# A pooling and SwiGLU layer on one core: all rows of x loaded first, still products on TensorE, low parts of the window means by TensorE and ScalarE

## The chip, the core and the metric

The kernel runs on one NeuronCore of a Trainium2 chip. The metric is the time of one execution on the device, in microseconds (us): the median of several executions. The engines are TensorE (PE; its weight loads are listed apart as PEld), VectorE (DVE), ScalarE (ACT), GpSimd (POOL) and SyncE (SP), which only issues transfers. A transfer (DMA) can be issued by SyncE or by GpSimd.

## The reference, cut to what matters

One layer is computed (DEPTH is 1, so the mixer is the pooling one, and the context tokens are never needed). x is 1024 x 1024, the hidden width F is 2816, everything is float32.

```
s_c = silu(c)
sh1, sc1, g1, sh2, sc2, g2 = split(s_c @ mod_w + mod_b, 6)
hx = x * (1 + sc1) + sh1
p_g = centred_window_mean(hx_g, w) - hx_g          # w = 2, 4, 8, 16; 256 columns each
ox = concat_g(p_g @ pool_w[g]) * pool_scale
x = layer_norm(ALPHA * x + g1 * ox, ln_g[0], ln_b[0])
h = x * (1 + sc2) + sh2
gt, up = split(h @ ffn_w_in, 2)
x = layer_norm(ALPHA * x + g2 * ((silu(gt) * up) @ ffn_w_out), ln_g[1], ln_b[1])
```

mod_w is 1024 x 6144, in six parts of 1024 columns (4 MB each) that the text calls by their names: sh1, sc1, g1, sh2, sc2, g2.

## The kernel before, in words

**Precision.** A product that has to keep float32 accuracy is made in one of two ways. A float32 product goes over TensorE in two passes (two matmul records for each). Or both operands are split into a high part, rounded to fp32r, and a low part, the rest; then three fp32r products of one pass each are summed (`mm3`, L260). `take_hi` (L265) makes a high part on ScalarE, `take_lo` (L268) the low part on VectorE by subtracting the high part.

**The front of the kernel** is everything ahead of the first product of the SwiGLU part (`gate_step`, L760). It goes as follows. The rows of x are in blocks of 128, `x0` to `x7`; `ORDER` puts blocks 1, 2, 3, 4 in half 0 and 5, 6, 7, 0 in half 1.

- *Window means.* For each half and each of 8 column blocks, `pool_inner` (L460) makes four float32 products of a block of x with a band matrix from the constants, and `pool_outer` (L465) one with the few halo rows, all into one PSUM bank (`ps_pt`). This gives mean minus row, transposed. `pool_hi` (L470, ScalarE) and `pool_lo` (L473, VectorE) then split the bank into `pt` high and low.
- *Row vectors of c.* A part of mod_w comes in eight slices of 128 x 1024 (`mod_load`, L294). VectorE adds slice times silu(c) into `acc` (`mod_add`, L490; the first of a part L488). Then eight narrow float32 products turn `acc` into a column (`mod_col`, L505), or two 512-wide ones spread it over all partitions (`g1_bank`, L547). Slices listed in `by_tensor` skip VectorE and go through TensorE as they are (`mod_whole`, L505).
- *Weights.* g1 times pool_scale, times 1 + sc1, is multiplied into pool_w on VectorE (`pool_w_weigh`, L569) and the result split (`wpsh`, `wpsl`).
- *Sums.* `pooled` (L261 to L263) makes for each block of rows and half of the columns 12 fp32r products of 256 columns: 16 such sums. `residual` (L607, VectorE) adds ALPHA x and frees the bank. Then per block: `mean`, `spread` (L628, ScalarE), `factor`, `norm` (L644, ScalarE), and `keep_row` stores the row.
- *Turning.* With all four blocks of half 0 normed, `turned` (L693) transposes them, `scaled_h` (L698, ScalarE) applies sc2 and sh2, `hidden_hi` and `hidden_lo` split. sc2 and sh2 are made as above (`finish_gain`, `finish_shift`, L675 to L680).
- *Gate.* `gate_load` brings slices of ffn_w_in, `gate_hi` (ScalarE) and `gate_lo` (VectorE) split them, and `gate_step` starts: 88 steps of six 512-wide fp32r products.

Behind the front come the rest of the SwiGLU part and the output products, by a long stream of 512-wide fp32r products that only TensorE bounds.

**What sets the order.** Each step is a job; `ORDER_OF_ISSUE` (L43) is a table that names the jobs in the order in which they are issued, and each engine runs its own instructions in that order. `PLACE_OF` (L111) says for each tile which buffer it takes, so which older tile must be done first. SyncE's queue runs in order as well: eight transfers are on their way at most, since each issue waits for the landing of the one eight places earlier. `warm_up` (L316) runs 12 float32 products of 128 columns on ones, ahead of everything.

Of the kernel before, what the change touches and what calls it, by code (L numbers as in the profile page):

```python
# [12 lines left out]
F32 = mybir.dt.float32  # L13
# [4 lines left out]
P = 128  # L18
# [14 lines left out]
WARM = 12  # L33
G2_AT = 5
BY_TENSOR = (0, 7)
# [28 lines left out]
gate_load.0 gate_load.1 gate_load.2 gate_load.3 gate_load.4 gate_load.5 pool_hi.10 pool_hi.8 mod_add.19 pool_inner.47
pool_outer.11 pool_inner.38 pool_hi.11 pool_inner.62 pool_inner.58 residual.1 pool_hi.9 mean.0 pooled.6 mod_add.20
pool_hi.14 spread.0 mod_add.21 residual.6 mod_add.22 pooled.4 pool_hi.15 factor.0 mod_col.1 mod_add.23 norm.0
residual.4 keep_row.0 mod_add.24 pooled.2 finish_gain.0 pooled.5 residual.2 mod_add.25 pooled.3 residual.5 residual.3
pooled.7 mean.2 mean.1 spread.2 mod_add.26 mod_whole.1 residual.7 spread.1 mean.3 factor.2 mod_whole.2 mod_add.27
norm.2 mod_add.28 pool_inner.48 spread.3 keep_row.2 pool_inner.49 pool_inner.51 pool_outer.12 pool_inner.50 factor.1
mod_col.2 pool_lo.10 norm.1 factor.3 pool_lo.11 norm.3 keep_row.1 pool_lo.14 pool_inner.52 pool_inner.53 turned.2  # L70
gate_hi.0 finish_shift.0 keep_row.3 turned.4 pool_lo.8 turned.3 scaled_h.2 pool_lo.9 turned.1 scaled_h.4 gate_lo.0
pool_inner.54 turned.0 turned.6 scaled_h.3 turned.7 scaled_h.0 pool_lo.15 turned.5 scaled_h.1 pooled.8 scaled_h.5
scaled_h.6 pooled.10 scaled_h.7 residual.8 hidden_hi.0 pooled.12 residual.10 gate_hi.2 hidden_lo.0 pooled.14
hidden_hi.1 residual.12 gate_hi.1 pool_inner.55 gate_lo.2 pool_outer.13 gate_step.0 gate_hi.4 residual.14 gate_step.1
# [1327 lines left out]
```

## Time and profile before

| | us |
|---|---|
| median of 3 runs | 742.33 (741.07 to 743.72) |
| profiled execution | 743.44 |
| its span, first to last instruction | 741.7 |
| TensorE busy in the span | 723.3 (98%) |
| VectorE, ScalarE, GpSimd busy | 556.9, 274.9, 171.9 |
| first gate product starts | 89.34 |
| last product of TensorE ends | 733.3 |
| mean granted TensorE clock | 0.971 |

How to read it: the page of the profile shows the span in 40 slices; TensorE is busy in nine tenths and more of all but the first slices. What matters for this change is the time before the first gate product, and there the stretches (busy time of an engine between two times, with the granted clock) and the timeline (instructions in order of time, merged where alike) are the views to use. The granted clock is 1.00 at 2.4 GHz and 0.50 at 1.2 GHz.

### The profile page before, as it was taken

To read this page: it belongs to the slowest core of one execution; us is meant where nothing else is said; L and a number is where in the kernel's file an instruction comes from. 1 tells how busy PE (TensorE), PEld (TensorE's weight loads), DVE (VectorE), ACT (ScalarE), POOL (GpSimd) and SP (SyncE) were. 2 spreads that over 40 slices of the span, in tenths; PEclk is the share of its full clock that TensorE was granted. 3 is DMA by queue.
4 is the path that set the end of the run, shared out by engine and by line. 5 is a ranking of instruction groups with operands and counts; after the bars stand their busy time and mean duration, and the time that the engine had idled before them with its cause. 6 is when DMAs were issued, how large, how long until landed. Compare 5 with 4: busy or idle time off the path is not lost.

```text
span 741.7 us, 9158 instructions
## 1 busy us (share of the span) xinstructions
PE 723.3 (98%) x3342; PEld 602.3 (81%) x3342; DVE 556.9 (75%) x677; ACT 274.9 (37%) x356; POOL 171.9 (23%) x131
## 2 busy tenths in 40 slices
PE   6999999999999999999999999999999999999995
PEld 5689988788888888888888888888888888888884
DVE  3788874749534788999999777975878679657896
ACT  0225954597441311311312212212557334335521
POOL 0000000005205835373733634600000000233100
PEclk7579999999999999999999999999999999999998
DMA  7999349566829589797987797456799856999612
GB/s 293 346 407 370 146 167 356 197 226 199 273 116 308 189 264 263 183 322 245 311 262 193 241 276 205 156 192 220 266 371 391 296 194 227 254 290 292 184 57 113
DMA packets 115202, 182.85 MB, mean 247 GB/s; under 512 B 7723, under 2 KB 66547, under 8 KB 114902
## 3 DMA queue, kind: packets, MB, share of 16 engines
q1 hardware_dynamic: 107894, 164.97, 64.4%
q0 software_dynamic: 7264, 17.30, 11.7%
q8 instruction: 26, 0.43, 0.2%
q14 instruction: 18, 0.15, 0.1%
HBM read 142.14 MB, written 51.64 MB: 261 GB/s over the span
## 4 chain that ended last, share of the span: by engine, by line
PE 92%; DMA 5%; DVE 2%; ACT 1%; issue 0%; SPq 0%; POOL 0%; POOLq 0%
PE ps_v L894 40%; PE ps_x L1105 16%; PE ps_gate L760 13%; PE ps_y L1105 12%; DMA wi<-in_ffn_w_in 2%; PE ps_pt L460 2%; PE ps_col L505 2%; PE ps_ox L261 1%; PE ps_ox L263 1%; PE ps_ox L262 1%; PE ps_h L693 1%; DMA x<-in_x 1%; DMA mw<-in_mod_w 1%; PE ps_pt L465 1%; DMA consts<-in_consts 1%; PE ps_psc L540 1%
## 5 line engine op out<-in xcount | busy, mean ns | idle before, releaser
L760 PE MATMUL ps_gate<-h,wih 128*128 128x512 f32 x352 | 109.3, 391 | 0.0
L894 PE MATMUL ps_v<-t,w0h 128*128 128x512 f32 x352 | 109.2, 391 | 0.0
L266 ACT CAST yhi<-yraw 128x1024 fp32r<-128x1024 f32 x77 | 78.7, 1051 | 79.6 <-DMA yraw<-in_ffn_w_out 17.0
L269 DVE TENSOR_TENSOR ylo<-yraw,yhi 128x1024 fp32r<-128x1024 f32 x77 | 91.6, 1219 | 18.2 <-ACT yhi L266 7.4
L961 POOL TENSOR_TENSOR s<-raw,raw 128x512 f32<-128x512 f32 x22 | 33.1, 1504 | 311.0 <-DMA raw<-in_ffn_w_in 301.9
L917 ACT ACTIVATE a<-a 128x512 f32<-128x512 f32 x22 | 13.9, 632 | 225.0 <-DVE a L916 225.0
L894 PEld LDWEIGHTS ps_v<-t,w0h 128*128 128x128 f32 x352 | 66.1, 188 | 14.5 <-issue 1.0
L760 PEld LDWEIGHTS ps_gate<-h,wih 128*128 128x128 f32 x352 | 65.7, 188 | 13.8 <-issue 0.5
L760 PE MATMUL ps_gate<-h,wil 128*128 128x512 f32 x176 | 68.5, 389 | 0.0
L894 PE MATMUL ps_v<-t,w0l 128*128 128x512 f32 x176 | 68.5, 389 | 0.0
L1105 PE MATMUL ps_x<-yhi 128*128 128x512 f32 x176 | 68.5, 389 | 0.0
L1105 PE MATMUL ps_x<-ylo,yhi 128*128 128x512 f32 x176 | 68.5, 389 | 0.0
L1105 PE MATMUL ps_x<-yhi,ylo 128*128 128x512 f32 x176 | 68.5, 389 | 0.0
L490 DVE SCALAR_TENSOR_TENSOR acc<-mw,s_col,acc 128x1024 f32<-128x1024 f32 x41 | 54.5, 1331 | 16.1 <-DMA mw<-in_mod_w 15.7
L1067 POOL DMA_DIRECT2D yraw<-in_ffn_w_out x22 | 18.7, 849 | 193.4 <-DMA yraw<-in_ffn_w_out 161.1
L894 PE MATMUL ps_v<-t,ws 128*128 128x512 f32 x264 | 63.4, 389 | 0.0
L894 PEld LDWEIGHTS ps_v<-t,ws 128*128 128x128 f32 x264 | 49.6, 188 | 10.3
L894 PE MATMUL ps_v<-h,w1h 128*128 128x512 f32 x176 | 54.2, 389 | 0.0
L894 PE MATMUL ps_v<-t,w1h 128*128 128x512 f32 x176 | 54.2, 389 | 0.0
L1105 PE MATMUL ps_y<-yhi 128*128 128x512 f32 x132 | 51.3, 389 | 0.0
L1105 PE MATMUL ps_y<-ylo,yhi 128*128 128x512 f32 x132 | 51.3, 389 | 0.0
L1105 PE MATMUL ps_y<-yhi,ylo 128*128 128x512 f32 x132 | 51.3, 389 | 0.0
(160 smaller groups left out, 1390.6 us busy)
## 6 DMA issues: line engine op xcount, KB each, us to landing
mw<-in_mod_w SPq DMA_DIRECT2D x48, 512.0 KB, 8.7
raw<-in_ffn_w_in SPq DMA_DIRECT2D x88, 256.0 KB, 5.6
wi<-in_ffn_w_in SPq DMA_DIRECT2D x22, 512.0 KB, 6.3
yraw<-in_ffn_w_out SPq DMA_DIRECT2D x44, 256.0 KB, 4.8
yraw<-ed SPq DMA_DIRECT2D x33, 256.0 KB, 6.0
ed<-in_ffn_w_out POOLq DMA_DIRECT2D x6, 1024.0 KB, 10.5
pd<-pk SPq DMA_DIRECT2D x11, 512.0 KB, 4.6
gd<-gk SPq DMA_DIRECT2D x11, 512.0 KB, 4.7
```

Of the source, the lines that this page charges most:

```text
L261: nc.tensor.matmul(ps, lh, rh, start=first, stop=False)
L266: nc.scalar.copy(hi, src)
L269: nc.vector.tensor_tensor(lo, src, hi.bitcast(F32), ALU.subtract)
L460: nc.tensor.matmul(pt_bank[half, ct][:, a:b], xr[ORDER[half][n]][:, ct * P : (ct + 1) * P], operand, start=n == 0, stop=False, skip_group_ ...
L490: nc.vector.scalar_tensor_tensor(acc, w, s_col[:, k : k + 1], acc, ALU.mult, ALU.add)
L505: nc.tensor.matmul(tiles["ps_col", j][:, n * WIDE : (n + 1) * WIDE], t[:, n * P : (n + 1) * P], by, start=first and n == 0, stop=last and ...
L760: nc.tensor.matmul(ps, x, y, start=k == n == 0, stop=k % 4 == 3 and n == 2, skip_group_check=k > 3)
L894: nc.tensor.matmul(ps, x, y, start=fresh and first, stop=last, skip_group_check=not fresh)
L917: nc.scalar.activation(a[:, 1], a[:, 1], ACT.Silu)
L961: nc.gpsimd.tensor_tensor(s, up1, up2, ALU.add)
L1067: nc.gpsimd.dma_start(raw[n][:, 1], ADDED[n // PAIRS](n % PAIRS), accum_op=ALU.add)
L1105: nc.tensor.matmul(ps, s[x][:, r * P : (r + 1) * P], t[y][:, d], start=fresh and j == m == 0, stop=j == PAIRS - 1 and m == 2, skip_group_c ...
```

## The change

All eight blocks of x are now loaded at the start, in turn with the slices of g1; then sc1, sc2 and sh2 follow. The small vectors, constants and halo rows move from SyncE's queue to GpSimd's. The warm-up becomes 64 fp32r products of 256 columns on a tile of ones (`still`), and 12 jobs `keep_warm` of four such products each stand among the first sums; their results are not used. The low part of all 16 window means is now made without VectorE: TensorE subtracts the high part in PSUM by a 512-wide fp32r product with a negated identity (`pool_less`), and ScalarE copies the rest out (`pool_rest`). pool_w is multiplied by g1 first (`pool_w_gain`, in two tiles of 128 x 256 for each job), and 1 + sc1 goes into the split (`pool_w_hi` on ScalarE, `pool_w_lo` on VectorE), 256 columns at a time. Slices 6 and 7 of sc1 now go through TensorE; slice 0 of sc2 and of sh2 no longer does. The table of the order and the table of buffers are new throughout, and all 16 `pooled` sums now stand ahead of the first `gate_step` (before: 12). The buffers that the later part takes in turn are sorted by when they were last used.

```diff
-WARM = 12
+WARM = 64
-BY_TENSOR = (0, 7)
+BY_TENSOR = (7,)
+LOW_BY_TENSOR = ((0, 1, 2, 3, 4, 5, 6, 7), (0, 1, 2, 3, 4, 5, 6, 7))
 ORDER_OF_ISSUE = """
-vector_rows.0 fill_constants.0 fill_ones.0 mod_start.0 warm_up.0 mod_load.0 load_consts.0 mod_load.1 load_x.0
...
+vector_rows.0 fill_constants.0 fill_ones.0 load_x.0 mod_start.0 negate.0 warm_up.0 load_consts.0 mod_load.0 load_x.1
...
+    minus = keep.tile([P, P], F32R, tag="minus", name="minus", bufs=1)
+    still = keep.tile([P, 256], F32R, tag="still", name="still", bufs=1)
...
         for _ in range(WARM):
-            nc.tensor.matmul(ps[:, :P], ones, ones, start=True, stop=True)
+            nc.tensor.matmul(ps[:, :256], still[:, :P], still, start=True, stop=True)
+    def keep_warm(n):
+        ps = bank(f"ps_still{n}")
+        for _ in range(4):
+            nc.tensor.matmul(ps[:, :256], still[:, :P], still, start=True, stop=True)
...
     def vector_rows(a, b, src):
-        nc.sync.dma_start(rows[a:b, :], src.rearrange("(j p) -> j p", p=P))
+        (nc.gpsimd if a else nc.sync).dma_start(rows[a:b, :], src.rearrange("(j p) -> j p", p=P))
...
+    def negate():
+        nc.scalar.activation(minus, ident, ACT.Copy, scale=-1.0)
+    def pool_less(half, ct):
+        nc.tensor.matmul(pt_bank[half, ct], minus, pt[half](0, ct), start=False, stop=True, skip_group_check=True)
+    def pool_rest(half, ct):
+        nc.scalar.copy(pt[half](1, ct), pt_bank.pop((half, ct)))
...
-    mod_columns(SC1, ())
+    mod_columns(SC1, (6, 7))
...
-    def pool_w_weigh(n):
+    def pool_w_gain(n):
+        w, g = tiles["wp", n // 2][:, n % 2 * 2 : n % 2 * 2 + 2, :], tiles["g1",][:, n * 256 : (n + 1) * 256]
+        for k in range(2):
+            nc.vector.tensor_tensor(w[:, k], w[:, k], g, ALU.mult)
+    def pool_w_hi(n):
+        nc.scalar.activation(wps[n // 4][0][:, n % 4], tiles["wp", n // 4][:, n % 4], ACT.Copy, scale=sc1[:, n : n + 1])
+    def pool_w_lo(n):
+        nc.vector.scalar_tensor_tensor(lo, tiles["wp", n // 4][:, n % 4], sc1[:, n : n + 1], hi.bitcast(F32), ALU.mult,
+                                       ALU.subtract)
...
-    mod_columns(SC2, (0,))
+    mod_columns(SC2, ())
```

What the tables do is seen in the rows of each engine. First SyncE's queue from its start, before (`mw_1_0` is slice 0 of sc1, `mw_2_0` slice 0 of g1, `x1` a block of x):

```order
L337 DMA rows_66<-in_c 8x128
L382 DMA acc2_156<-in_mod_b 1x1024
L294 DMA mw_1_0_172<-in_mod_w 128x1024
L356 DMA consts_72<-in_consts 128x288
L294 DMA mw_1_1_175<-in_mod_w 128x1024
L353 DMA x1_177<-in_x 128x1024
L294 DMA mw_1_2_179<-in_mod_w 128x1024
L337 DMA rows_66<-in_mod_b 48x128
L337 DMA rows_66<-in_ln_g 8x128
L337 DMA rows_66<-in_ln_b 8x128
L353 DMA x2_190<-in_x 128x1024
L294 DMA mw_1_3_192<-in_mod_w 128x1024
```

The same queue after the change:

```order
L353 DMA rows_66<-in_c 8x128
L369 DMA x1_159<-in_x 128x1024
L372 DMA consts_74<-in_consts 128x288
L301 DMA mw_2_0_231<-in_mod_w 128x1024
L369 DMA x2_233<-in_x 128x1024
L301 DMA mw_2_1_237<-in_mod_w 128x1024
L369 DMA x3_240<-in_x 128x1024
L301 DMA mw_2_2_243<-in_mod_w 128x1024
L369 DMA x4_246<-in_x 128x1024
L301 DMA mw_2_3_251<-in_mod_w 128x1024
L369 DMA x5_253<-in_x 128x1024
```

x and g1 alternate, sc1 has moved behind both, and the small rows are gone from this queue. Next TensorE near the end of the means of half 0, before (`ps_pt0_7` is the bank of half 0, column block 7; `x3`, `x4` are blocks of half 0, `x5` of half 1):

```order
L460 MATMUL ps_pt0_7_271<-consts_72,x3_194 128x143
L460 MATMUL ps_pt0_7_271<-consts_72,x4_199 128x135
L465 MATMUL ps_pt0_7_271<-consts_72,halo_207 128x2x8
L547 MATMUL ps_g1_0_375<-acc2_156,ones_69 128x512
L547 MATMUL ps_g1_1_381<-acc2_156,ones_69 128x512
L460 MATMUL ps_pt1_7_387<-consts_72,x5_263 128x136
L460 MATMUL ps_pt1_3_390<-consts_72,x5_263 128x130
```

The same place after it (L500 is `pool_inner`, L505 `pool_outer`, L517 `pool_less`, L336 `keep_warm`):

```order
L517 MATMUL ps_pt0_2_295<-pt0_01_328,minus_70 128x512
L517 MATMUL ps_pt0_1_274<-pt0_00_323,minus_70 128x512
L517 MATMUL ps_pt0_4_337<-pt0_02_361,minus_70 128x512
L500 MATMUL ps_pt0_5_353<-consts_74,x2_233 128x135
L500 MATMUL ps_pt0_5_353<-consts_74,x3_240 128x135
L500 MATMUL ps_pt0_5_353<-consts_74,x4_246 128x131
L505 MATMUL ps_pt0_5_353<-consts_74,halo_248 128x2x8
L336 MATMUL ps_still0_376<-still_71 128x256 x4
L336 MATMUL ps_still1_383<-still_71 128x256 x4
L500 MATMUL ps_pt1_7_390<-consts_74,x5_253 128x136
```

The 512-wide subtractions and the still products stand among the narrow window products, and the sums of g1 come later. Last ScalarE around its first weights of the gate (`wih0_0`), before:

```order
L628 ACTIVATE sq4_659,mv4_528<-x4_199,mv4_528 128x1024
L629 ACTIVATE mv4_528<-mv4_528,eps_70 128x1
L644 ACTIVATE x2_190<-x2_190,mv2_593 128x1024
L644 ACTIVATE x4_199<-x4_199,mv4_528 128x1024
L266 CAST wih0_0_697<-wi_0_0_482 128x1024
L698 ACTIVATE h32_0_1_715<-ps_h0_2_692,shift_75,gain_74 128x512
```

After it (L273 is `take_hi`, L690 the `spread`, L706 the `norm`):

```order
L520 CAST pt1_10_668<-ps_pt1_1_411 128x512
L273 CAST wih0_0_815<-wi_0_0_685 128x1024
L690 ACTIVATE sq4_834,mv4_739<-x4_246,mv4_739 128x1024
L691 ACT_TABLE_LOAD
L691 ACTIVATE mv4_739<-mv4_739,eps_72 128x1
L690 ACTIVATE sq1_866,mv1_688<-x1_159,mv1_688 128x1024
L691 ACTIVATE mv1_688<-mv1_688,eps_72 128x1
L690 ACTIVATE sq2_893,mv2_670<-x2_233,mv2_670 128x1024
```

The cast of the first gate weights now stands ahead of all four spreads of half 0, where it stood behind their norms.

## Rows read from the trace of the kernel before

**Rows 1.** Stretches of TensorE: from:to us, busy (instructions), granted clock, DMA share, GB/s

```profile
89.34:101.70 12.36, 12.36 (x55) 1.00 0.32 116
101.70:107.47 5.77, 5.77 (x50) 1.00 0.98 311
107.47:733.30 625.83, 625.58 (x2776) 1.00 0.76 241
6.31:9.04 2.73, 0.00 (x1) 1.00 0.97 344
11.27:22.00 10.73, 8.57 (x33) 0.50 0.95 358
22.00:42.90 20.90, 20.68 (x68) 0.50 1.02 378
46.58:53.00 6.42, 6.42 (x54) 1.00 1.03 409
```

**Rows 2.** Timeline row of the warm-up; its weight loads: ns min/median/max, starts in us

```profile
1.06 5.10 PE L320 MATMUL ps_warm<-ones 128*128 128x128 f32 x24 [1.06 <-DVE ones L310]
...
L320 PEld LDWEIGHTS ps_warm<-ones x3: 333/333/333, 4.8 to 5.3; 128*128 128x128 f32 x3
...
L320 PEld LDWEIGHTS ps_warm<-ones x3: 192/192/257, 5.5 to 5.8; 128*128 128x128 f32 x3
```

**Rows 3.** Timeline of TensorE: start us, us, line, names, shapes, records merged

```profile
36.79 0.82 PE L460 MATMUL ps_pt<-consts,x 128*128 128x135 f32 x2
...
38.08 2.15 PE L460 MATMUL ps_pt<-consts,x 128*128 128x132 f32 x8
...
42.93 3.78 PE L547 MATMUL ps_g<-acc,ones 128*128 128x512 f32 x4
46.50 2.03 PE L460 MATMUL ps_pt<-consts,x 128*128 128x136 f32 x16
...
50.12 0.49 PE L460 MATMUL ps_pt<-starts,x 128*128 128x128 f32 x2
...
50.86 0.49 PE L460 MATMUL ps_pt<-starts,x 128*128 128x128 f32 x2
...
76.67 1.89 PE L505 MATMUL ps_col<-ones,acc 128*128 128x64 f32 x16
...
80.94 1.91 PE L693 MATMUL ps_h<-ident,x 128*128 128x128 f32 x16
```

**Rows 4.** Timeline of ScalarE between the first spread and the gate weights

```profile
61.80 1.28 ACT L629 ACT_TABLE_LOAD   x1
...
72.77 1.13 ACT L628 ACTIVATE sq<-x,mv 128x1024 f32<-128x1024 f32 x1
...
74.23 1.23 ACT L644 ACTIVATE x<-x,mv 128x1024 f32<-128x1024 f32 x1
...
76.82 2.36 ACT L644 ACTIVATE x<-x,mv 128x1024 f32<-128x1024 f32 x2
...
80.02 5.45 ACT L698 ACTIVATE h<-ps_h,shift,gain 128x512 f32<-128x512 f32 x8
...
91.02 2.02 ACT L266 CAST wih<-wi 128x1024 fp32r<-128x1024 f32 x2
```

**Rows 5.** Groups of VectorE, 0 to 110 us: line, names xcount | busy us, mean ns | idle before

```profile
L490 DVE SCALAR_TENSOR_TENSOR acc<-mw,s_col,acc 128x1024 f32<-128x1024 f32 x29 | 37.1, 1282 | 9.8 <-DMA mw<-in_mod_w 9.4
L473 DVE TENSOR_TENSOR pt<-ps_pt,pt 128x512 fp32r<-128x512 f32 x16 | 10.5, 683 | 2.9 <-ACT pt L470 2.9
```

**Rows 6.** Timeline of SyncE's issues: start us, us, what, count

```profile
35.55 20.00 SPq L294 DMA_DIRECT2D mw<-in_mod_w  x16
56.50 11.83 SPq L294 DMA_DIRECT2D wi<-in_ffn_w_in  x6
```

**Rows 7.** Tile wi, 50 to 70 us: from issue to landing

```profile
DMA to landing us min/median/max: 8.5/10.2/11.8
```

More of the change, by code (lines that the diff above doesn't have):

```diff
@@ L64 @@
[L64 to L73, printed above, removed]
@@ new lines @@
+pooled.11 keep_row.2 norm.3 residual.10 residual.12 turned.0 keep_row.3 gate_hi.2 turned.1 residual.14 turned.3
+scaled_h.0 residual.15 gate_lo.2 turned.2 scaled_h.1 hidden_hi.0 turned.4 turned.5 residual.13 hidden_lo.0 scaled_h.2
+turned.6 scaled_h.3 turned.7 hidden_hi.1 residual.11 gate_step.0 scaled_h.6 residual.8 hidden_lo.1 scaled_h.7
+gate_step.1 hidden_hi.3 gate_step.2 hidden_lo.3 scaled_h.4 scaled_h.5 gate_step.3 residual.9 hidden_hi.2 mean.4 mean.5
+hidden_lo.2 gate_hi.4 gate_step.4 gate_hi.3 gate_lo.4 gate_step.5 gate_hi.1 gate_lo.3 gate_step.6 mod_load.32
@@ new lines @@
+x2 sq6 wi_4_0 wil6_0 gk6 wi_10_0 wih10_1
+psc mw_3_3 h0_00 pk10
+mw_2_1 mw_4_3 wi_0_0 pk0 mw_0_7 wi_6_1 wi_8_1 pk8 t4_01
+x3 wi_3_0 gk2 gk4 wih9_0 t4_11
+mw_2_2 pt1_00 wil2_0 wih4_1 wil8_1 pk9
+x4 wi_3_1 wil5_0 wih8_0 gk7 t1_10
+halo mw_3_4 h0_01
+mw_2_3 mw_4_4 wi_1_1 wq_0 wih7_1 wil10_0
+x5 wih10_0 gk10
+mw_2_4 pt1_13 acc0 wi_7_1 wil9_0 t3_00
+x6 t3_01
+ends wpsh0 wih2_1 gk3 gk5 raw1_0
+mw_2_5 mw_4_5 wi_2_0 gk0 wih5_0 ws1_0
+x7 t2_01
+mw_2_6 pt1_02 mw_0_4 wil4_1 wi_9_0 t1_00
+x0 t2_00
+mw_2_7 mw_4_6 h32_0_3 wil10_1
@@ L402, in trunk_kernel @@
     job(load_consts, slice(2 * BAND, 4 * BAND))
-    for k in (6, 7):
-        job(mod_load, SC1, k)
-    job(mod_start, G1)
     job(load_scale)
-    for k in range(KT):
-        job(mod_load, G1, k)
+    job(mod_load, G1, 1)
+    job(load_x, 3)
+    job(mod_load, G1, 2)
+    job(load_x, 4)
+    job(mod_load, G1, 3)
+    job(load_x, 5)
+    job(mod_load, G1, 4)
+    job(load_x, 6)
+    job(mod_load, G1, 5)
+    job(load_x, 7)
+    job(mod_load, G1, 6)
+    job(load_x, 0)
+    job(mod_load, G1, 7)
+    job(mod_load, SC1, 0)
+    job(mod_load, SC1, 1)
+    job(mod_load, SC1, 2)
+    job(mod_load, SC1, 3)
     for j in range(2):
         job(load_pool_w, j)
-    for i in ORDER[1]:
-        job(load_x, i)
-    for j in (SC2, SH2):
-        for k in range(KT):
-            job(mod_load, j, k)
+    job(mod_load, SC1, 4)
+    job(mod_load, SC1, 5)
+    job(mod_load, SC1, 6)
+    job(mod_load, SC1, 7)
+    job(mod_load, SC2, 0)
+    job(mod_load, SC2, 1)
+    job(mod_load, SC2, 2)
+    job(mod_load, SC2, 3)
+    job(mod_load, SC2, 4)
+    job(mod_load, SC2, 5)
+    job(mod_load, SC2, 6)
+    job(mod_load, SC2, 7)
+    job(mod_load, SH2, 0)
+    job(mod_load, SH2, 1)
+    job(mod_load, SH2, 2)
+    job(mod_load, SH2, 3)
+    job(mod_load, SH2, 4)
+    job(mod_load, SH2, 5)
+    job(mod_load, SH2, 6)
+    job(mod_load, SH2, 7)
     for kh in range(2):
@@ L531, in mod_columns @@
             job(mod_col, j, not by_tensor)
-    sc1 = small("sc1", (P, KT))
-    mod_columns(SC1, ())
-    job(mod_col_done, SC1, 1.0, sc1)
     def scale_bank(h):
@@ L1015, in trunk_kernel @@
         used = {taken[kind, name] for name in LASTING[kind] + UNDER_WAY[kind]}
-        free[kind] = deque(n for n in range(count) if n not in used)
+        free[kind] = deque(sorted((n for n in range(count) if n not in used), key=lambda n: turn.get((kind, n), -1)))
     first, second = column_half(0), column_half(1)
```

263 lines of the change are left out of this document (130 added, 133 removed).

## The prediction

> **What bounds the kernel now.** I read the stretches of TensorE first. From 107.47 to the last product at 733.30 it is busy for 625.58 of 625.83 us at the full clock [rows 1]. In that part nothing is to be had but fewer products, and the change alters none of them. So what counts is when the dense stream begins and what still has to be put into it. Now the first gate product starts at 89.34. From 101.70 to 107.47 four sums of `pooled`, 48 products, stand in the stream [rows 1]. The change puts all 16 sums ahead of the gate, so its first gate product has to be compared with 89.34 + 5.77 = **95.1**: earlier than that is a gain, one for one, later a loss.
>
> What bounds the front? The clock first. In the warm-up a weight load takes 333 ns up to 5.3 us and 192 ns from 5.5 [rows 2], so the clock came up about 4.5 us after the warm-up's start at 1.06. After it TensorE idles, and at 9.04 the clock falls; from 11.27 to 42.90 it is 0.50, though TensorE is busy for 20.68 of the last 20.90 us there [rows 1]. The four 512-wide products of g1 [rows 3] are the last thing before it rises, and from 46.58 it stays at 1.00, over narrow window products too [rows 1]. So some 35 us of first sums run at 1.2 GHz, and TensorE itself is the limit of the front up to 46 us. From there on the sums of mod_w on VectorE (1.28 us a slice [rows 5]) and the spreads and norms on ScalarE hold it.
>
> **The change part by part.** I follow TensorE through the new order. At 2.4 GHz a window product (two passes) takes 2.03 / 8 = 0.25 us, and one together with a halo product 50.86 - 50.12 = 0.74; at 1.2 GHz these are 2.15 / 4 = 0.54 and 38.08 - 36.79 = 1.29 [rows 3]. A 256-wide fp32r product takes 5.77 / 48 = 0.12 and a 512-wide one 12.36 / 54 = 0.23 [rows 1].
>
> - Warm-up: 64 products at 0.12, doubled while the clock is low. If it starts at 1.06 and the clock rises 4.5 us later as now, 19 run slow and 45 fast (5.4 us): it ends at 11.0. That costs no useful time, since x lands near there now too: its first products start at 11.27 [rows 1].
> - Window means of both halves, 48 x 0.25 + 16 x 0.74 = 23.8 us.
> - The two rows of pool_scale and the two of g1: eight 512-wide passes. Four take 3.78 at the low clock [rows 3], so 1.9 at the high one, together 3.8.
> - 12 of the 16 subtractions ahead of the sums of sc1: 12 x 0.23 = 2.8. Still products 0 to 8: 36 x 0.12 = 4.3. The two small transposes of vectors: 0.5, an estimate. Waits for x and for the vectors: 1.0, chosen between 0 and the 4 to 5 us that the first product waits now between 6.31 and 11.27 [rows 1]; nearer to 0, because the warm-up now covers that time.
>
> Sum: 11.0 + 23.8 + 3.8 + 2.8 + 4.3 + 0.5 + 1.0 = 47.2.
>
> - Three times eight narrow products for sc1, 1.8 each by the 1.89 of one set [rows 3]: 5.4, to 52.6. Then VectorE adds the bias, ScalarE and VectorE split 256 columns: 1.0, by half of the 0.68 of a 512-wide step [rows 5] for each: 53.6. The last subtractions and still products lie in that gap and cost nothing.
> - 14 sums of 12 x 0.12 = 1.44: 20.2, to 73.8. Slice 7 of sh2 and the two last column sets, 3 x 1.8: 79.2. Two more sums 2.9: 82.1.
> - Turning: eight sets at 1.91 / 4 = 0.48: 85.9. Beside it the way over the other engines for the first step: two sets 1.0, `scaled_h` 5.45 / 8 = 0.7, `hidden_hi` 1.0 [rows 3, 4], `hidden_lo` 1.2 (a little under the 1.28 of the same size [rows 5]): 86.0.
>
> So the first gate product starts at **86.0**, 9.1 us ahead of 95.1.
>
> **The other engines against that.** VectorE loses 16 low parts of 0.683, 10.5 us [rows 5]. It keeps 29 slices up to sh2 (26 adds and 3 first ones), since two of sc1 leave and one each of sc2 and sh2 come. Behind the last slice of g1 it has 18 adds (23.0), three first slices (3.8 at most), two rows of g1 and eight residuals at 0.68 (6.8), 16 steps of 256 columns at about 0.4 (6.4) and some 2.5 of small ones: 42.5. Slices come every 20.00 / 16 = 1.25 us [rows 6]; g1's last is the sixteenth large transfer, so at about 27 if the first comes near 7, an estimate. VectorE is then through at 69.5, ahead of TensorE at 79.2, and the low parts are no longer on the path.
>
> ScalarE takes 16 casts more and eight short splits for two long ones, before 56 us, where its trace has room. What is new there is a wait: the cast of the first gate weights stands ahead of all four spreads, and these, four norms and the turning queue behind it. The weights are issued at 56.50 and land 8.5 to 11.8 us later [rows 6, 7], so between 65.0 and 68.3. At the late end: cast 1.0, a table load 1.3, four spreads at 74.23 - 72.77 = 1.46, four norms at 1.2: 68.3 + 12.9 = 81.2; then a cast 1.0, two `scaled_h` 1.4, `hidden_hi` 1.0, `hidden_lo` 1.2: 85.8 [rows 4]. At the early end it is 82.5. It just fits under the 86.0, so I add nothing, but a later landing costs one for one.
>
> The bytes ahead of the gate are the same. GpSimd's eleven small issues hide behind the warm-up, if they land by the time x2 and x3 are used up. Sorting the free buffers changes which buffer comes next and no product.
>
> The new time is 743.44 - 9.1 = 734.3 against the profiled execution; that one lies 1.1 above the median, so I put the median at 742.33 - 9.1 = **733.2**. What a measurement of this kernel can tell from no change is about 0.3%, so 740.1 to 744.6 counts as the same.
>
> **The rivals.**
>
> *The clock does not stay up* (slower). The first sums are narrow products with halts for x, for vectors from GpSimd's queue and for ScalarE's casts. At 1.2 GHz the same kind of products, 20.68 us busy of 20.90, did not bring the clock back; only the 512-wide ones of g1 came ahead of the rise [rows 1, 3]. If it falls while TensorE waits for the vectors and returns behind g1's rows, 12 pairs with a halo product cost 0.55 more each, 28 window products 0.29, eight subtractions 0.23, eight still products 0.12 and g1's rows 1.9: 19.4 us. The first gate product comes at 105.4 and the time is 752.6. It decides from 9.1 us of extra time on: about as much as all sums from the vectors to still product 0 at the low clock. The Trainium skill, page "TensorE: Matmul & The Clock Gate", section "A second HAM failure mode: psum-queue depth-cycling", says that a kernel stepping through PSUM banks can leave TensorE idle for short moments so often that its clock goes back and forth. By that rule this rival would hold. Here the stretch from 46.58 to 53.00 speaks against it: the same window products, bank after bank, at 1.00 throughout [rows 1]. I give this rival 14 in 100.
>
> *It falls for a while only.* Back with the first subtractions (10 window products and 3 pairs slow): 4.6 us, 737.8. Back with still product 0 (16, 8 pairs, five subtractions): 10.2 us, 743.4. 17 in 100, some 10 of them above the bound for faster.
>
> *A wait takes its place later.* The gate weights of later pairs queue behind the stores of normed rows and the slices of sh1 on SyncE; or the first ones land later than 68.3. Then TensorE, with the gate 9 us earlier, stands for them. Each landing that is 1 us late costs 1 us; I take 4 to 5 us, one landing time's spread of 3.3 and a cast: 738. The trace has TensorE waiting for nothing there now (625.58 of 625.83 [rows 1]). 8 in 100.
>
> *The forecast*, the clock up from the warm-up on: 61 in 100. Its own range is 729 to 737: with no waits for x, ScalarE at its early end and shorter halts 4 us better; with 4 us of waits, the upper bound above, that much worse.
>
> **How the numbers follow.** Faster: 61 + 10 + 7 = 78 in 100; the same: 7 + 1 = 8; slower: 14. The range of 728 to 745 leaves out the slower rival and a small tail below, 18 in 100.
>
> **What would show it.** In the changed kernel's trace: the granted clock at 1.00 from about 5.5 us without a fall; the warm-up's end near 11; the column sums of sc1 ended near 53; TensorE almost without idle time from there; the first gate product at 86, ScalarE's cast of the first gate weights before 69.3; no idle TensorE behind the gate's start. The forecast is wrong if the clock is at 0.50 for more than 15 us of the first sums, if TensorE waits for `pooled`'s weights or for residuals between 53 and 82, or if it idles behind the first gate product.

## The result and the profile after

The changed kernel takes 735.62 us (median of 5; 734.89 to 738.04), the kernel before, measured beside it, 742.33: ratio 0.9914, 95% interval 0.9896 to 0.9933. So it is faster, by 6.7 us in the medians; 9.1 was forecast. The profiled executions have spans of 741.7 and 734.2, 7.5 apart. The clock does not come out alike in every execution of one kernel, and the medians hold all of them: of the changed kernel's five, that with a mean granted clock of 0.992 has a span of 736.3, those at 0.995 to 0.997 have 733.1 to 734.2.

The warm-up's products in the stretches 4 to 5 us and 6 to 10.9 us (duration in ns, min/median/max; first and last start in us):

```profile
L330 PE MATMUL ps_warm<-still x7: 415/415/415, 3.7 to 5.0; 128*128 128x256 f32 x7
L330 PE MATMUL ps_warm<-still x42: 279/283/283, 5.7 to 10.7; 128*128 128x256 f32 x42
```

So the first products of the warm-up run slow, the clock comes up near 5.3 us, and from there on it stays up; before, it fell at 9.04 and was low up to 46.58 [rows 1]. Stretches of the changed kernel (from:to, length, busy us and instructions of PE, PEld, DVE, ACT, POOL, granted clock, DMA share, GB/s):

```profile
5.32:46.14 40.82, 39.89 (x266) 34.08 (x265) 23.51 (x28) 18.63 (x36) 3.12 (x7) 1.00 1.02 387
46.14:53.86 7.72, 7.72 (x66) 7.55 (x65) 3.59 (x7) 1.97 (x5) 0.00 (x0) 1.00 1.03 410
53.86:82.30 28.44, 28.44 (x242) 28.44 (x241) 25.23 (x55) 16.75 (x27) 0.00 (x0) 1.00 0.71 255
82.30:86.80 4.50, 4.08 (x34) 3.30 (x32) 4.29 (x6) 4.01 (x7) 0.00 (x0) 1.00 1.01 317
86.80:725.55 638.75, 638.31 (x2828) 526.57 (x2828) 484.19 (x562) 243.83 (x305) 167.01 (x124) 1.00 0.76 240
```

TensorE has hardly a gap from the warm-up to the end: 39.89 us of the 40.82 up to the columns of sc1, all of the 36.16 behind. Its timeline, and some rows of VectorE and ScalarE (start us, us, engine, line, names, shape, records; idle time before, and its releaser):

```profile
1.19 9.74 PE L330 MATMUL ps_warm<-still 128*128 128x256 f32 x64 [1.19 <-DVE still L319]
27.32 1.21 PE L336 MATMUL ps_still<-still 128*128 128x256 f32 x8
42.71 3.59 PE L336 MATMUL ps_still<-still 128*128 128x256 f32 x28
46.14 3.68 PE L560 MATMUL ps_col<-s_col,mw 128*128 128x64 f32 x32
49.66 1.95 PE L560 MATMUL ps_col<-ones,acc 128*128 128x64 f32 x16
51.41 1.68 PE L336 MATMUL ps_still<-still 128*128 128x256 f32 x12
52.93 1.09 PE L517 MATMUL ps_pt<-pt,minus 128*128 128x512 f32 x4
53.86 0.28 PE L268 MATMUL ps_ox<-wpsh,pt 128*128 128x256 f32 x1
...
75.78 3.68 PE L560 MATMUL ps_col<-ones,acc 128*128 128x64 f32 x32
82.23 2.84 PE L755 MATMUL ps_h<-ident,x 128*128 128x128 f32 x24
85.27 0.66 PE L755 MATMUL ps_h<-ident,x 128*128 128x128 f32 x4 [0.20 <-DVE x L669]
86.12 0.66 PE L755 MATMUL ps_h<-ident,x 128*128 128x128 f32 x4 [0.20 <-ACT h L760]
86.80 0.74 PE L822 MATMUL ps_gate<-h,wih 128*128 128x512 f32 x2
...
51.74 1.28 DVE L545 SCALAR_TENSOR_TENSOR acc<-mw,s_col,acc 128x1024 f32<-128x1024 f32 x1
66.78 2.60 DVE L545 SCALAR_TENSOR_TENSOR acc<-mw,s_col,acc 128x1024 f32<-128x1024 f32 x2
69.30 0.57 DVE L685 TENSOR_SCALAR mv<-mv 128x1 f32<-128x1 f32 x4
69.79 6.31 DVE L545 SCALAR_TENSOR_TENSOR acc<-mw,s_col,acc 128x1024 f32<-128x1024 f32 x5
64.66 1.05 ACT L273 CAST wih<-wi 128x1024 fp32r<-128x1024 f32 x1 [7.54 <-DMA wi<-in_ffn_w_in]
69.68 1.15 ACT L690 ACTIVATE sq<-x,mv 128x1024 f32<-128x1024 f32 x1 [3.97 <-DMA wi<-in_ffn_w_in]
```

The first gate product stands at 86.80, 8.3 us ahead of the 95.1 with which the prediction compares it. Behind it the dense stream takes 638.75 us, against 643.96 - 5.77 = 638.19 before [rows 1], and the tail behind the last product 734.2 - 725.55 = 8.65, against 8.4. So 8.3 - 0.56 - 0.25 = 7.5 us are left, which is the difference of the spans.

### The profile page after: what moved, and what is told of

Same layout as the page of the kernel before. It is cut to its first block, busy times and chain, and to the rows that moved or that the text cites. A ratio compares the mean times of both kernels' runs of the same rounds, so it can differ in the third digit from the quotient of the medians.

```text
span 734.2 us, 9409 instructions
## 1 busy us (share of the span) xinstructions
PE 722.6 (98%) x3446; PEld 604.1 (82%) x3446; DVE 546.3 (74%) x668; ACT 287.9 (39%) x382; POOL 174.5 (24%) x143
## 3 DMA queue, kind: packets, MB, share of 16 engines
HBM read 142.14 MB, written 51.64 MB: 264 GB/s over the span
## 4 chain that ended last, share of the span: by engine, by line
PE 90%; DMA 4%; DVE 4%; ACT 1%; issue 1%; POOL 0%; SPq 0%; DVEq 0%; ACTq 0%; POOLq 0%
PE ps_v L956 41%; PE ps_x L1167 16%; PE ps_y L1167 12%; PE ps_gate L822 11%; DMA mw<-in_mod_w 2%; PE ps_pt L500 2%; DVE h L915 2%; PE ps_col L560 2%; PE ps_ox L268 1%; PE ps_ox L269 1%; PE ps_ox L270 1%; DMA consts<-in_consts 1%; DVE acc L545 1%; PE ps_still L336 1%; DMA rows<-in_ln_b 1%; PE ps_pt L505 1%
## 5 line engine op out<-in xcount | busy, mean ns | idle before, releaser
L273 ACT CAST yhi<-yraw 128x1024 fp32r<-128x1024 f32 x77 | 78.7, 1051 | 77.3 <-PE ps_x L1167 21.0
## 6 DMA issues: line engine op xcount, KB each, us to landing
mw<-in_mod_w SPq DMA_DIRECT2D x48, 512.0 KB, 10.2
```

The lines of the kernel that those rows point to most:

```text
L273: nc.scalar.copy(hi, src)
```

## The experiments

All twelve runs in one table. The ratio is to the kernel before, with its 95% interval. "Gate" is the start of the first gate product in the profiled execution; the kernels marked * have the old order, with four sums still behind it, so 5.77 us have to be added to compare.

| kernel | us | ratio | gate |
|---|---|---|---|
| changed kernel | 735.62 | 0.9914 (0.9896 to 0.9933) | 86.80 |
| e1_no_still | 732.3 | 0.9873 (0.9850 to 0.9896) | 86.52 |
| e2_short_warm_up | 738.74 | 0.9954 (0.9940 to 0.9968) | 89.96 |
| e3_low_by_vector | 734.38 | 0.9903 (0.9881 to 0.9924) | 85.37 |
| e4_warm_up_alone * | 742.37 | 1.0006 (0.9993 to 1.0019) | 88.25 |
| e5_clock_held_old_order * | 744.49 | 1.0038 (1.0021 to 1.0054) | 90.92 |
| e6_x_late | 741.8 | 1.0000 (0.9982 to 1.0017) | 94.02 |
| e7_small_loads_by_sync | 742.24 | 1.0010 (0.9997 to 1.0023) | 94.45 |
| e8_clock_held_less * | 740.76 | 0.9980 (0.9964 to 0.9996) | 85.10 |
| e9_sync_later_transposes | 738.13 | 0.9947 (0.9927 to 0.9967) | 90.28 |
| b1_mixed | 730.6 | 0.9862 (0.9842 to 0.9882) | 82.40 |
| b2_chain | 731.69 | 0.9864 (0.9840 to 0.9889) | 87.00 |
| b3_short_still | 735.76 | 0.9912 (0.9889 to 0.9935) | 83.78 |

My theory at the start was the prediction's: the clock is the gain. The rivals: the new order of the loads, or the low parts taken off VectorE.

### The clock, in the new order

**e2_short_warm_up**

```diff
-WARM = 64
+WARM = 12
-            nc.tensor.matmul(ps[:, :256], still[:, :P], still, start=True, stop=True)
+            nc.tensor.matmul(ps[:, :P], ones, ones, start=True, stop=True)
```

> The changed kernel with the old warm-up: 12 products of 128 columns in place of 64 of 256; all else as in the changed kernel. My theory, that the clock kept up from the warm-up on is the gain: TensorE idles from about 6.2 to 10.9 us, the clock falls near 9, and the first sums run at 1.2 GHz until denser work brings it back. If that is the first subtractions (10 us of work before them) about 10 us are lost: 746 us; if it is the rows of g1 or the long row of still products, 17 to 20 us: 753 to 756 us. The rival, that the order of the loads is the gain and the front waits for loads anyway until 46 us: at most 3 us lost, 739 us or less.

0.0040 of 742.3 us more than the changed kernel, 3 us: the rival's number, but not for the rival's reason, since TensorE waits for no load behind 10.74 us. Its stretches (columns as above):

```profile
6.80:10.20 3.40, 0.17 (x2) 0.08 (x1) 0.17 (x1) 0.00 (x0) 0.67 (x3) 1.00 1.01 388
10.20:20.44 10.24, 9.70 (x27) 6.24 (x28) 3.64 (x4) 4.10 (x8) 0.95 (x2) 0.50 1.03 370
20.44:49.31 28.87, 28.87 (x192) 25.15 (x191) 20.77 (x25) 14.72 (x28) 0.00 (x0) 1.00 1.04 402
```

The clock falls as foreseen while TensorE stands, but it is back at 20.44, before the first subtraction, with nothing but window means, the rows of pool_scale and small transposes behind it. I had not expected that: before, the window means ran at 0.50 from 22.00 to 42.90 [rows 1].

**e1_no_still**

```diff
-    for n in range(12):
+    for n in range(0):
         job(keep_warm, n)
...
```

(The twelve jobs are taken out of the table of the order as well.)

> The changed kernel without its 48 still products (the warm-up stays). In the changed kernel's trace 36 of them stand where TensorE would otherwise wait for loads (8 from 27.3 to 28.4 us, 28 from 42.7 to 46.1), and 12 stand between the column sums of sc1 and the first sum of pooled (51.4 to 52.9). My theory, that the full clock is the gain and that TensorE must not stand still before the column sums: an idle stretch of about 3.4 us opens from 42.7, the clock falls near 45 to 46 as it fell in the kernel before 2.7 us after its idle began, 48 column products are then loaded at 333 instead of 192 ns (5.4 us become about 9), the first sums run slow until it rises again (2 us more), 1.5 us are saved behind the columns: about 740 us, with the granted clock at 0.50 for 5 to 10 us. The rival, that the still products only fill and do nothing for the clock: no fall, and 1.5 us less than the changed kernel: 734 us.

3 us faster than the changed kernel. In the profiled execution the clock did fall, but early, behind a wait for the constants (11.14 to 11.82), not at the columns:

```profile
11.82 0.72 PE L499 MATMUL ps_pt<-consts,x 128*128 128x136 f32 x4 [0.68 <-DMA consts<-in_consts]
46.05 3.79 PE L559 MATMUL ps_col<-s_col,mw 128*128 128x64 f32 x32 [0.22 <-ACT pt L519]
53.48 0.39 PE L268 MATMUL ps_ox<-wpsl,pt 128*128 128x256 f32 x1 [0.64 <-DVE wpsl L638]
```

```profile
10.92:15.72 4.80, 4.12 (x18) 2.27 (x18) 1.33 (x2) 3.58 (x8) 0.63 (x2) 1.00 1.04 354
15.72:22.55 6.83, 6.21 (x29) 5.93 (x28) 5.23 (x6) 0.31 (x1) 0.00 (x0) 0.50 1.04 410
```

Though that wait and the low clock made it 3.4 us late (its first halo product starts at 22.72, the changed kernel's at 19.28), it reaches the columns at 46.05, as the changed kernel does. Its three other executions, at a mean clock of 0.997, have spans of 729.5 to 730.5. So the 36 still products ahead of the columns did not fill waits: TensorE had work, and they pushed it back. The 12 behind the columns did fill one for the most part: without them TensorE waits at 53.48 for the low part of the weights, and its first sum runs only 0.4 us earlier.

### The clock and the warm-up, in the old order

**e4_warm_up_alone**, the kernel before with this edit:

```diff
-WARM = 12
+WARM = 64
-            nc.tensor.matmul(ps[:, :P], ones, ones, start=True, stop=True)
+            nc.tensor.matmul(ps[:, :256], still[:, :P], still, start=True, stop=True)
...
```

> The kernel before with the new warm-up alone (64 products of 256 columns from one tile of ones); order, loads and low parts as before. My theory, that the clock is of use only with the new order of loads: the warm-up bridges the 5 us to the first x, but g1's rows wait for the last slices of mod_w (VectorE has them at 41.7 us), so TensorE runs dry on the way there and gains at most the 3 us by which g1's rows now end behind that: 739 to 742 us. The rival, that the clock alone is the whole gain, in any order: 735 to 737 us.

No change in the median. The clock does not hold: in the old order TensorE waits for the vector rows and then for three blocks of x, 0.75, 0.49, 1.40 and 1.40 us, and from 17.86 on it is low for 27.3 us, where before it was low from 9.04 to 46.58:

```profile
4.21:17.86 13.65, 10.05 (x78) 9.21 (x77) 5.60 (x7) 0.21 (x1) 0.00 (x0) 1.00 1.01 375
17.86:45.16 27.30, 25.79 (x80) 19.15 (x81) 20.34 (x23) 7.11 (x14) 0.00 (x0) 0.50 1.00 371
```

**e5_clock_held_old_order** and **e8_clock_held_less** add seven rows of still products to e4:

```diff
+    def keep_warm(n, count):
+        ps = bank(f"ps_still{n}")
+        for _ in range(count):
+            nc.tensor.matmul(ps[:, :256], still[:, :P], still, start=True, stop=True)
+    for n, count in enumerate((6, 4, 11, 11, 16, 36, 44)):     # e8: (6, 4, 11, 8, 14, 18, 8)
+        job(keep_warm, n, count)
...
```

> The kernel before with the new warm-up and seven rows of still products (6, 4, 11, 11, 16, 36 and 44 of them) at the places where its TensorE would wait at the full clock: before the transposes, before each of x2 to x4, before the first halo products, before the column sums of sc1 and before the rows of g1. Order, loads and low parts as before. It asks for the clock alone, now that the warm-up alone did not hold it (it fell at 17.9 us and came back at 45.2). My theory, that the clock is of little use without the new order of loads, because g1's rows wait for slices that VectorE has summed at 41.7 us: the rows end near 43.7 instead of 46.6, and of these 2.9 us something stays behind VectorE: 739.5 to 742 us. The rival, my forecast's own reading that the clock is the first limit of the front: 736 us or less.

> The kernel before with the clock held, again, since the run before it overshot: its last two rows of still products (36 and 44) kept TensorE busy to 31.4 and 46.3 us, when VectorE had the sums that follow at 29.1 and 38.9. Now 6, 4, 11, 8, 14, 18 and 8 still products. Without the overshoot g1's rows can start near 39 us instead of 42.9 and end near 41 instead of 46.5. If the clock alone is of little use in the old order, since the second half's x lands only at 42 to 45 us and the slices of sc2 and sh2 up to 67 us (my theory): 738.5 to 741 us. The rival, that a held clock gives the whole gain once it costs nothing: 736 us or less.

e5 asked the question badly: its rows were too long, and g1's rows started at 46.30, after VectorE had the sum at 38.9. e8 mends that. Its g1 rows start at 39.52 instead of 42.93 [rows 3], its first gate product is 4.2 us ahead of before's 89.34, and 1.5 us of time (0.0020) are won. Of the rest, waits behind the gate's start took a part: 0.7 us for a sum of slices near 125, and 0.9 us for low gate weights at 204. In its trace the clock is not held throughout either: it is low from 32.22 to 39.05 (the rows stand in the last section). That fall cost little, since g1's rows need a sum that VectorE ends only at 29.89 + 9.20 = 39.09:

```profile
29.89 9.20 DVE L501 SCALAR_TENSOR_TENSOR acc<-mw,s_col,acc 128x1024 f32<-128x1024 f32 x7
```

Of its ten executions one has a mean clock of 0.998, and a span of 737.3; another at 0.991 has 737.5; the median span of the kernel before, measured beside them, is 740.9. So a clock held up, or nearly so, gives 1.5 us in the old order by the medians, 3.6 us in that one execution, at the price of some still products; it is not the gain by itself.

### Loads

**e6_x_late** (table of the order: `load_x.4` to `load_x.7` moved to stand ahead of `pool_inner.60`)

```diff
-load_x.4
...
-load_x.7
...
+load_pool_w.0 load_x.4 load_x.5 load_x.6 load_x.7 pool_inner.60
```

> The changed kernel with the second half's four tiles of x loaded behind the eight slices of g1, four of sc1 and half of pool_w, near their old place, instead of in turn with g1's slices; no other order is touched. If x first is what lets TensorE run without a halt (my theory): it stands from about 28 us, when the first half's sums are done, to 35 to 37, when those tiles land, and the first gate product comes 6 to 9 us later than in the changed kernel: 741 to 745 us. The rival, that the columns of sc1 wait for their own slices anyway and these now come earlier: at most 3 us lost, 739 us or less.

The whole gain is gone, as my theory said. The waits in its timeline are smaller than I had thought, 2.0 us:

```profile
30.19 1.21 PE L336 MATMUL ps_still<-still 128*128 128x256 f32 x8
32.56 0.69 PE L500 MATMUL ps_pt<-consts,x 128*128 128x136 f32 x4 [1.17 <-DMA x<-in_x]
33.76 0.49 PE L500 MATMUL ps_pt<-consts,x 128*128 128x131 f32 x2 [0.27 <-DMA x<-in_x]
35.02 0.51 PE L500 MATMUL ps_pt<-ends,x 128*128 128x129 f32 x2 [0.55 <-DMA x<-in_x]
```

They are followed by a low clock from 35.36 to 38.77, 1.7 us more. Of the 7.2 us by which its gate is late, 2.9 are there ahead of these waits (30.19 against the changed kernel's 27.32): the clock fell at 14.88 to 21.71, behind a 0.46 us wait for the constants, which the edit does not touch. So 4.3 us are x's in this execution. Whether the rest of the medians' 6.4 (0.0086) is x's too isn't shown; the four executions of e6 at a mean clock of 0.995 have spans of 737.8 to 740.6, the changed kernel's at 0.995 to 0.997 have 733.1 to 734.2.

**e7_small_loads_by_sync** and **e9_sync_later_transposes**

```diff
-        (nc.gpsimd if a else nc.sync).dma_start(rows[a:b, :], src.rearrange("(j p) -> j p", p=P))
+        nc.sync.dma_start(rows[a:b, :], src.rearrange("(j p) -> j p", p=P))
...
# e9 as well, in the table of the order:
-pool_inner.10 to_columns.1 pool_inner.1
+pool_outer.1 to_columns.1 pool_less.0
```

> The changed kernel with all its small loads (rows of vectors, constants, halo rows, the scale row, the bias row) on SyncE's queue again. The prediction costed this part of the change at nothing. If that holds: 734.6 to 737 us, no difference to the changed kernel that shows. The rival, that eleven issues of 0.33 to 0.45 us in front of the large loads push x and the slices back: 3 to 5 us later, 739 to 741 us.

> The small loads on SyncE's queue again (742.2 us when that was the only edit), now with one more: the transposes of the 64 vector rows stand behind the first halo products on TensorE. In the run before, TensorE stood 5.2 us for these rows (they landed near 21 us), and its clock fell from 20.3 to 27.1. If that wait and the fall that follows it are the whole price (my theory): 735.5 to 738 us, the first halo products waiting 1 us or so. If the large loads, pushed back behind the small ones, are the price (the rival that I wrote down for that run): it stays at 740 us or more.

e7 loses 7 us (0.0096), more than the rival's price, but not in the rival's way: neither x nor a slice is waited for. One wait does it, and the clock behind it (first e7's timeline, then its stretch, then e9's):

```profile
21.50 0.35 PE L359 MATMUL ps_cols<-ident,rows 72*128 72x72 f32 x1 [5.22 <-DMA rows<-in_ln_b]
```

```profile
20.27:27.10 6.83, 5.60 (x25) 5.41 (x25) 5.11 (x5) 0.00 (x0) 0.00 (x0) 0.50 1.03 379
```

```profile
15.21:22.03 6.82, 6.82 (x29) 6.19 (x29) 3.86 (x3) 1.98 (x6) 0.00 (x0) 0.50 0.94 337
```

The row starts 21.50 - 16.51 = 4.99 us later than the changed kernel's: 4.29 by the longer wait (5.22 against 0.93), 0.7 by a later start (11.71 against 11.01). The low clock adds about half of the 5.60 us that TensorE is busy there, 2.8. Together that is 7.8, and the gate is 94.45 - 86.80 = 7.65 late. With the transposes further back (e9) the wait is gone, and 0.0063 or 4.7 us of the 7 come back. In its place stand 1.5 us for the constants and again a low clock, 3.4 us. Its one execution at a mean clock of 0.997 has a span of 733.9, as the changed kernel's; so by this one execution, which isn't traced, the large loads, pushed back, cost next to nothing. The median, 738.13, lies just above the 738 that I gave.

### Low parts

**e3_low_by_vector**

```diff
-LOW_BY_TENSOR = ((0, 1, 2, 3, 4, 5, 6, 7), (0, 1, 2, 3, 4, 5, 6, 7))
+LOW_BY_TENSOR = ((), ())
...
```

> The changed kernel with the low parts of the window means on VectorE again, 16 subtractions of 0.68 us, at the places where ScalarE now takes them out; the 16 products with the negative identity go. My theory, that VectorE has room for most of them and that this part of the change is worth little: the sums of sc1's slices come 1 to 3 us later by them, TensorE's four subtractions behind the columns (0.9 us) are saved: 735.5 to 738 us. The rival, that the low parts on VectorE are what the change mainly takes off the path: back near the time before, 741 to 743 us.

Not slower at all: 734.38, with an interval that overlaps the changed kernel's, and in the trace the gate is 1.4 us earlier:

```profile
43.88 3.68 PE L559 MATMUL ps_col<-s_col,mw 128*128 128x64 f32 x32
50.68 0.28 PE L267 MATMUL ps_ox<-wpsh,pt 128*128 128x256 f32 x1
51.64 0.39 PE L268 MATMUL ps_ox<-wpsl,pt 128*128 128x256 f32 x1 [0.69 <-DVE wpsl L638]
85.37 0.73 PE L821 MATMUL ps_gate<-h,wih 128*128 128x512 f32 x2
```

The columns of sc1 start 2.3 us earlier than at 46.14, though the front began 0.35 us later: 12 subtractions of 0.23 are gone from ahead of them. VectorE had the room, but for the wait of 0.69 us at 51.64, which e1 has as well (0.64), and the subtractions loaded the engine that was the limit. Of the 2.3 us some 0.7 are lost again at the turning, where TensorE waits 0.58 us for ScalarE.

### Putting it together

**b1_mixed**

```diff
-LOW_BY_TENSOR = ((0, 1, 2, 3, 4, 5, 6, 7), (0, 1, 2, 3, 4, 5, 6, 7))
+LOW_BY_TENSOR = ((), (0, 1, 2, 3, 4, 5, 6, 7))
-    for n in range(12):
-        job(keep_warm, n)
# in the table of the order:
-pool_inner.10 to_columns.1 pool_inner.1
+pool_outer.1 to_columns.1 pool_hi.2
-pool_less.0 pool_hi.2 mod_add.3 pool_inner.27 pool_outer.6 pool_rest.0
+pool_hi.2 mod_add.3 pool_inner.27 pool_outer.6 pool_lo.0
...
```

> The changed kernel without the still products, with the low parts of the first half's means on VectorE again (those of the second half stay on TensorE and ScalarE), and with the transposes of the 64 vector rows moved behind the first halo products, so that TensorE does not wait for these rows at 15.6 us. My theory now, that TensorE itself is the limit from the warm-up to the first sum of pooled and that still products and subtractions lie on the path: the columns of sc1 start when their slices land, near 41 to 42 us instead of 46.1, the first sum near 49 instead of 53.9, and of these 4 to 5 us the chain over VectorE and ScalarE keeps some back: 729 to 731.5 us. The rival, that behind the still products another limit (loads, VectorE's sums) stands close: no better than without still products, 732 us or more.

730.6 us. By the ratios that is 0.0138 or 10.2 us less than the kernel before and 0.0052 or 3.9 us less than the changed kernel: the lowest median of all, though its interval overlaps with those of e1 and b2. Its timeline:

```profile
40.80 3.75 PE L558 MATMUL ps_col<-s_col,mw 128*128 128x64 f32 x32 [0.56 <-DMA mw<-in_mod_w]
47.91 0.38 PE L266 MATMUL ps_ox<-wpsh,pt 128*128 128x256 f32 x1 [0.59 <-ACT wpsh L628]
82.40 0.73 PE L817 MATMUL ps_gate<-h,wih 128*128 128x512 f32 x2
```

Now TensorE waits at the columns for a slice, so the loads have become the limit there. Two more versions went after what was left.

**b2_chain** (b1 with these moves in the table of the order)

```diff
-mod_add.16 mod_col_done.0 mod_add.17
...
+pool_w_lo.7 mod_add.16 mod_add.17
...
-mod_add.24 mod_whole.2 mod_add.25 gate_hi.0 mean.3 mean.1 pooled.9 mean.0 mean.2 spread.3
+mean.3 mean.1 mean.0 mean.2 pooled.14 spread.3 spread.0 spread.1 spread.2 mod_add.24 mod_whole.2 mod_add.25
...
```

> The kernel without still products and with the first half's low parts on VectorE (b1_mixed, 730.6 us) with four moves on VectorE and ScalarE: two sums of sc2's slices go behind the splitting of pool_w (TensorE waited 1.3 us there for sc1 and for the low parts), the four means go ahead of two sums of sh2's slices, the cast of the first gate weights goes behind the four spreads, and the factors go between the sums. My theory: TensorE's first sum starts at about 47 instead of 48 to 49 us, and the chain of spreads and norms, which stood 0.5 us ahead of the gate, no longer binds: first gate product at 80.5 to 81.3 instead of 82.4, 728.5 to 729.8 us. The rival, that VectorE's sums of sc2 and sh2, now begun later, end later and take the place of both waits: no change, 730 to 731 us.

**b3_short_still** (b2 with `WARM = 70` and two jobs `keep_warm` ahead of `mod_whole.0`)

> The last kernel (b2_chain, 731.7 us) with 8 still products between the last subtraction and the columns of sc1, where its TensorE stood 1.4 us for a slice and its clock fell from 45.7 to 55.9, and with 70 warm-up products in place of 64, because it also stood 0.6 us for constants at 10.8 and its clock fell from 15.0 to 18.4. My theory, that still products pay just where TensorE would otherwise stand, and cost nothing there: the clock stays up in nearly every execution, 728.5 to 730.5 us, with the first gate product near 81. The rival, that the clock falls there whatever stands in the gap, or that the products lie on the path as those of the changed kernel did: 731.5 us or more.

Neither beats b1: b2 can't be told from it, and b3 is slower, by 0.0050 or 3.7 us. b2's profiled execution, the slowest of its six, shows a new trap, a fall of the clock at the columns, the very one I had forecast for e1 (a row of its timeline, then a stretch):

```profile
42.98 4.61 PE L558 MATMUL ps_col<-s_col,mw 128*128 128x64 f32 x32 [1.35 <-DMA mw<-in_mod_w]
```

```profile
45.68:55.92 10.24, 10.24 (x46) 9.85 (x46) 5.73 (x12) 4.25 (x10) 0.00 (x0) 0.50 1.03 410
```

b3 puts still products into that wait. In its profiled execution the clock is up throughout, and it still has a span of 730.7 against b1's 728.8:

```profile
41.43 1.22 PE L334 MATMUL ps_still<-still 128*128 128x256 f32 x8 [0.71 <-ACT pt L518]
42.49 3.68 PE L558 MATMUL ps_col<-s_col,mw 128*128 128x64 f32 x32
74.46 2.00 PE L558 MATMUL ps_col<-ones,acc 128*128 128x64 f32 x16 [0.78 <-DVE acc L543]
```

The still products had to wait for a PSUM bank that ScalarE was reading, and pushed the columns to 42.49 (b1: 40.80, behind a warm-up 0.5 us shorter); and VectorE's sums, moved back in b2, are now 0.78 late. Both rivals hold in part. Four of b3's six executions have a mean clock of 0.989 to 0.992 and spans of 733.9 to 735.5. Where the clock fell in these isn't seen, since only one execution is traced.

## Why the prediction was right, and where it was not

By its steps, with the rows of the changed kernel:

- *The dense stream can't change, and its start is what counts*: right. 638.75 us, 0.56 longer than before, of which 0.4 are two waits for low gate weights, at 125.85 and 198.93; a small part of the rival of a later wait, which I had left out of the sum.
- *The clock up from the warm-up on*: right in this trace, 1.00 from 5.32 with no fall. The warm-up ends at 10.93 (11.0 forecast).
- *To the columns of sc1*: 46.14 (47.2 forecast), ended at 51.61 (52.6).
- *The split behind the columns takes 1.0, and the last subtractions and still products lie in that gap and cost nothing*: the first sum starts at 53.86 (53.6 forecast), 2.25 us behind the columns, but the 1.1 us won before hide a term that was too small. The split itself took 1.9 us, as e1 shows, where TensorE waits for the low part up to 53.48: between the bias and the split VectorE has a sum of 1.28 us in its queue (51.74). The still products in the gap cost some 0.4.
- *Sums and columns to 82.1*: 82.30.
- *VectorE through with the slices at 69.5*: 69.79 + 6.31 = 76.10, 6.6 us later. The last columns start at 75.78 and do not wait, so it was in time, but with little of the room that the prediction saw there.
- *Turning to 85.9*: 86.80; two waits of 0.20 for PSUM banks, and some 0.4 us by restarts behind them.
- *ScalarE's cast of the first gate weights before 69.3*: 64.66. The spreads began at 69.68, near the 69.3 of the late end, but not for the cast, which was done at 65.71 though the row still names its weights as the releaser: the means on VectorE came only at 69.30, behind two sums.

So the gate came 0.8 us later than forecast, the stream lost 0.56 and the tail 0.25; that is the 1.6 us between 9.1 and 7.5. The rest, to 6.7, is how single executions lie to the medians: the one before is 1.1 above its median, the one after (736.0) 0.4.

The size came out near, in part by errors that cancel, but the reading of the cause was too simple. **"What bounds the front? The clock first"** does not stand alone. A warm-up alone gave nothing (e4), a clock held up for the most part in the old order 1.5 us (e8, where VectorE's sum at 39.09 is the next limit), and with the old warm-up in the new order 3 of the gain are lost, not 10 to 20 (e2), since the clock comes back by itself at 20.44. I read these runs so that loads and clock go together: TensorE is fed without halts, and then the clock mostly stays. The rival *the clock does not stay up* was priced at 19.4 us for a fall that lasts to g1's rows; falls seen in the new order lasted 3.4 to 10.2 us and cost about half of that. It came true in a small form, in some executions.

Two parts that I had priced at nothing, or as cover, were neither. The small loads on GpSimd's queue were right to cost nothing, but I did not see that without them the changed order would lose 7 us (e7). The low parts, "no longer on the path" of VectorE, moved work to the engine that was the path: TensorE's 12 subtractions, which stand in my sum with 2.8 us, bought nothing that shows (e3). The same holds for still products 0 to 8, priced at 4.3 and measured at 1.14 + 3.34 = 4.5 us: without them the kernel is 3 us faster (e1). I had added both to the path and not asked whether the path was better without.

What was not taken apart: the new split of pool_w, the slices of sc1 that TensorE now takes, the buffers, and the rest of the new order. What stays open: why the clock falls in some executions of one kernel and not in others, and why it came back at 20.44 in e2, over window means and the rows of pool_scale, and not over the same work in the kernel before. On the first, the Trainium skill, page "TensorE: Matmul & The Clock Gate", section "What's actually happening", says that the same kernel shows different numbers of slow products at its start from run to run. The mean clocks of b3's executions, 0.989 to 0.997, differ from run to run as well, but they do not say at which products, and no run here shows the cause.

## What to carry to other kernels

Ask of every instruction that is added to keep an engine awake, or to relieve another, whether the engine it lands on is the one that sets the end; take it out once and measure. A small load at the wrong place in a queue costs its wait on the in-order engine and then half of the low clock that may follow, so look where each small tile is first needed as closely as at the large ones. Parts of a change may be worth nothing alone and much together, or the other way round: undo them one at a time.

## What the runs showed of the hardware

- Short waits can be followed by a low clock, and not at once. In the profiled executions of e1, e6, b2 and e9 TensorE stood 0.68, 0.46, 0.58 and 1.5 us for the constants right behind the warm-up, and the clock fell at 15.72, 14.88, 14.96 and 15.21. In those of the changed kernel, e3, b1 and b3 it did not stand there, and the clock stayed at 1.00; waits of 0.93 and 1.00 us for the vector rows near 16 us (changed kernel, e3) were followed by no fall.
- The clock can fall with no wait near it. In e8 (stretches, columns as above)

```profile
4.91:32.22 27.31, 26.33 (x192) 23.09 (x190) 16.54 (x18) 5.08 (x12) 0.00 (x0) 1.00 0.97 357
32.22:39.05 6.83, 6.83 (x27) 6.22 (x27) 6.65 (x7) 2.03 (x4) 0.00 (x0) 0.50 1.06 387
29.00:32.22 3.22, 3.22 (x21) 2.27 (x20) 3.18 (x4) 0.31 (x1) 0.00 (x0) 1.00 1.01 408
```

  TensorE is busy for all of the 3.22 us before the fall and of the 6.83 us of low clock, with narrow columns, the rows of pool_scale and window means. The Trainium skill, page "TensorE: Matmul & The Clock Gate", section "A second HAM failure mode: psum-queue depth-cycling", puts such swings down to short idle moments between groups of products. No idle moment shows in this stretch (the profile models the ends of products, so a very short one could be hidden), so that rule alone isn't shown to explain the fall; and the changed kernel steps through all eight PSUM banks with the clock at 1.00 from 5.32 to 725.55.
